# Swapping the fifth and sixth block products of a pair, and moving part of a split from ScalarE to VectorE

## The chip, the cores and the metric

The kernel runs on one core of a Trainium2 chip. The metric is the device time of one execution in microseconds (us). The core has five engines with a queue each, worked off in order: TensorE (PE; its weight loads are shown apart as PEld), VectorE (DVE), ScalarE (ACT), GpSimd (POOL) and SyncE (SP, which only issues DMAs here). Engines wait for one another by semaphores. Each instruction stands in its engine's queue in the order in which the program wrote it, in the stages that matter here, so an instruction that waits holds up all that is behind it on its engine.

## The reference

One decoder block on a sequence of 2048 positions and 1024 channels:

```
h = RMSNorm(x) * (1 + scale(c)) + shift(c)
x_rnn, z_rnn, q, k, v, z_attn, g_r, g_a = split(h @ w_in)          # eight times 1024 columns
xc = causal_conv4(x_rnn);  r, i = sigmoid gates of xc by blocks of 128
a = exp(-8 r softplus(-lam));  hr = scan: hr[t] = a[t] hr[t-1] + sqrt(1 - a^2)[t] i[t] xc[t]
y_rnn  = (hr * silu(z_rnn)) @ w_out_rnn
y_attn = (mixture of three dilated window attentions of rotated q, k and v * silu(z_attn)) @ w_out_attn
out = RMSNorm(x + gate(c) * ((sigmoid(g_r) y_rnn + sigmoid(g_a) y_attn) @ w_o))
```

Results are wanted in float32 accuracy.

## The kernel before, in words

**Split operands.** Every float32 operand of a large matmul is stored as a high part (a rounded copy, float32r) and a low part (operand minus high part), and a product is three matmuls: high x high, high x low, low x high (`mm3`). A high part is made by a copy on ACT (`hi_act`, L162) or DVE (`hi_dve`, L165), a low part by a subtraction on POOL (`lo_pool`, L168) or DVE (`lo_dve`, L171).

**Pairs of column blocks.** The input projection is done in two halves of 1024 positions (f = 0, 1). In each, after the values v, 28 pairs of 128 columns of `w_in` follow (`pair_order`, L1209): pairs 0, 2, 5, 8, 10, 13, 16 and 18 belong to the recurrence (one block of x_rnn and one of z_rnn), those between and up to 21 are gates or plain parts of q and k, 22 to 27 are the rotated and the rest of the plain parts. A pair is a 2 x 2 block product, computed by `strassen` (L351) with seven block products instead of eight. Each block product (`prod`) is twelve matmuls of 128 x 512 into one PSUM tile. Their left operands are made from the pair's raw blocks a11, a21, a22, a12 and two sums s1, s2 (by DVE, `sums`); their right operands B11, T2, T3, T1, B21, T4, B22 are made once for all pairs. In order:

| product | left | right | PSUM tile | what follows |
|---|---|---|---|---|
| 1 | a11 | B11 | X | the pair before gets its seventh product |
| 2 | s2 | T2 | Z | u1 = copy of X (ACT, L390), u2 = Z + u1 (DVE, L391) |
| 3 | a21 | T3 | W | u3 = W + u2 (DVE, L396) |
| 4 | s1 | T1 | V | block (1,1) = V + u3 |
| 5 | a12 | B21 | X again, added | block (0,0) = X |
| 6 | a22 | T4 | Y | block (1,0) = Y + u3 |
| 7 | s2' | B22 | V again, added | block (0,1) = V + u2, one product into the next pair |

The copy u1 is made by DVE (L388) in pairs 5 and 22 of the first half (`COPIED`), else by ACT. Product 5 writes into X and so waits for u1; product 7 writes into V and waits for V + u3.

**The order of the work.** A counter `n_prod` is raised by each product. After a product, `run_late` issues the steps that are due at this count, then `pump` the events of operand making; then `strassen` goes on (u1 and u2 come behind both, after product 2). Operand events (`operand_events`, L267) run four products ahead: a pair's sums are made after product 3 of the pair before, and then one operand is split per product, on ACT and POOL, in the order a11, s2, a21, s1, a12, a22, s2'. The raw blocks are loaded up to six products ahead by SP into five tiles. For the first 20 pairs the split operands of the first half are also stored in HBM (`sD`, seven slots a pair) by DMAs of ACT's queue and loaded from there in the second half, so that the second half splits only those of pairs 20 to 27.

**A finished block's steps.** What is done with a block is counted from the product that finished it (`steps_after`, L232). A gate block gets a sigmoid one product later and a multiplication or a store behind it. Of a recurrent pair, z blocks (1,·) get sigmoid and multiplication (`z_part`, L948); the two x blocks (0,·) get, counted from block (0,0)'s product, for the first and seven later for the second: tap at 0 (ACT), taps at 1 (DVE), split at 2 (ACT, POOL), gates at 5 (PE, six matmuls), sigmoids at 6 (ACT), decay at 7 (POOL, DVE), exponentials at 8 (ACT), root at 9 (DVE), square root at 10 (ACT), scan at 11 (DVE: L1016 multiplies t by gi, L1017 scans), finish and store at 12 (`x_part`, L961: ACT's copy of the last state, L1020, DVE's L1022, SP's store). These reach two and three pairs on.

**Rotary tables.** `piece` (L1082) makes four pieces per half at counts `PIECES` (L43): a copy (DVE, L1087), four transposes 3 products later (PE, L1092), copying out and a store 4 products later. The rotated blocks get shuffle, sines, addition and store with lags that grow with the block's place (`x` in `rotated`).

**Attention and output products.** Attention is woven with the output projections: eight jobs (`steps`) of 64 `mm3` each, four with the recurrence's result (yaT) and then four with attention's (oT). A job's eight input tiles are split by `split_y` (L1768), the high part on ACT, the low part on POOL or DVE, around the end of the job before. Job 0 is split before attention starts, jobs 1 to 4 run in attention, jobs 5 to 7 behind it; then comes the last projection, with seven products per pair again.

Of the kernel before, what the change touches and what calls it, by code (L numbers as in the profile page):

```python
# [14 lines left out]
AF = mybir.ActivationFunctionType  # L15
# [9 lines left out]
NB = 4  # L25
# [10 lines left out]
MORE = 0.8  # L36
FIRST = 4.0
REBUILT = 20
COPIED = (5, 22)
NEG = 1e30  # L40

TABLES = 24
# [50 lines left out]
def decoder_block(ctx, tc, x, c, positions, g_norm, w_mod, b_mod, w_in, b_gate, conv_w, conv_b,  # L93
                  w_a, b_a, w_x, b_x, lam, w_out_rnn, w_out_attn, w_o, g_final, cst, out):
    nc = tc.nc
# [65 lines left out]
    def hi_act(o, i):  # L161
        nc.scalar.activation(o, i, AF.Copy)  # L162
# [49 lines left out]
    def split_s(src):  # L212
        t = s_tile([P, 2, KH, P])
        hi_act(t[:, 0], src)
        lo_pool(t[:, 1], src, t[:, 0])
        return t
# [5 lines left out]
    def run_late(n):  # L222
        for fn in (*late.pop(n, ()), *after_prod.pop(n, ())):
            fn()
        pump()
# [41 lines left out]
    def operand_events(x, pieces):  # L267

        load, v = block_loads(pieces), {}
        tt = nc.vector.tensor_tensor  # L270

        def raw(name, i, half):
            v[name] = load(i, half)

        def split(i, name):
            first[7 * x + i] = t = split_s(v[name])
            if x < REBUILT:
                kept.append((7 * x + i, t))
            if len(kept) > 3 or x >= REBUILT and kept:
                k, t2 = kept.pop(0)  # L280
                nc.scalar.dma_start(sD[k], t2[:].bitcast(F32))

        def sums():
            for name in ("s1", "s2"):
                v[name] = T(wq, [P, KH, P], F32, name, bufs=1)[:]
            tt(v["s1"], v["a21"], v["a22"], ALU.add)
            tt(v["s2"], v["s1"], v["a11"], ALU.subtract)  # L287

        yield -6, lambda: raw("a11", 0, 0)
        yield -5, lambda: raw("a21", 1, 0)  # L290
        yield -4, lambda: raw("a22", 1, 1)
        yield -1, lambda: raw("a12", 0, 1)
        yield 0, sums
        yield 0, lambda: split(0, "a11")
        yield 1, lambda: tt(v["a21"], v["a11"], v["a21"], ALU.subtract)
        yield 1, lambda: split(1, "s2")
        yield 2, lambda: split(2, "a21")
        yield 3, lambda: split(3, "s1")
        yield 4, lambda: split(4, "a12")
        yield 5, lambda: tt(v["s2"], v["a12"], v["s2"], ALU.subtract)  # L300
        yield 5, lambda: split(5, "a22")
        yield 6, lambda: split(6, "s2")

    first, events = {}, []
# [46 lines left out]
    def strassen(f, key, done):  # L351

        up = pu[0]
        x = pair_id[key]
        if f and x == 0:
            for _ in range(NS):
                load_next()
        n_op = iter(range(7 * x, 7 * x + 7))

        def take():  # L360
            if f and x < REBUILT:
                return (f, *loaded.pop(0))
            i = next(n_op)
            return f, i, first.pop(i)

        def prod(ps, b, first, last, op=None):
            f, i, s = op or take()
            bh, bl = B[b]
            for k in range(KH):
                mm3(ps[:], s[:, 0, k, :], s[:, 1, k, :], bh[:, k, :], bl[:, k, :],  # L370
                    first=first and k == 0, last=last and k == KH - 1, skip_group_check=True)
            n_prod[0] += 1
            if f:
                used.add(i)
                while n_loaded[0] - NS in used:
                    load_next()
            run_late(n_prod[0])

        X = T(pj, [P, CH], F32, "X", bufs=2)
        prod(X, "B11", True, False)  # L380
        last_product()
        Z = T(pj, [P, CH], F32, "Z")
        prod(Z, "T2", True, True)
        u1 = T(up, [P, CH], F32, "u1", bufs=1)
        u2 = T(up, [P, CH], F32, "u2", bufs=2)
        with tc.high_priority():
            if not f and x in COPIED:
                nc.vector.tensor_copy(u1[:], X[:])  # L388
            else:
                nc.scalar.activation(u1[:], X[:], AF.Copy)  # L390
            nc.vector.tensor_tensor(u2[:], Z[:], u1[:], ALU.add)  # L391
        W = T(pj, [P, CH], F32, "W")
        prod(W, "T3", True, True)
        u3 = T(up, [P, CH], F32, "u3", bufs=1)
        with tc.high_priority():
            nc.vector.tensor_tensor(u3[:], W[:], u2[:], ALU.add)  # L396
        V = T(pj, [P, CH], F32, "V")
        prod(V, "T1", True, False)
        done(1, 1, V, u3)
        prod(X, "B21", False, True)  # L400
        done(0, 0, X, None)
        Y = T(pj, [P, CH], F32, "Y")
        prod(Y, "T4", True, True)
        done(1, 0, Y, u3)
        op = take()

        def last():
            prod(V, "B22", False, True, op)
            done(0, 1, V, u2)
        behind.append(last)  # L410
# [629 lines left out]
    def rotary_tables(rp, f):  # L1040
# [41 lines left out]
        def piece(q, i):  # L1082

            def repeat():
                src = v[("co", "an")[i]]
                v["rep"] = raw_tile([P, 4, 8, 16]) if f else T(rp, [P, 4, 8, 16], F32, "ev", bufs=3)
                nc.vector.tensor_copy(v["rep"][:], src[:, 4 * q : 4 * q + 4, :].unsqueeze(2).broadcast_to([P, 4, 8, 16]))  # L1087

            def turn():
                v["pt"] = T(pg, [P, 4, P], F32, "pg")  # L1090
                for r in range(4):
                    nc.tensor.transpose(v["pt"][:, r, :], v["rep"][:, r].rearrange("p a b -> p (a b)"), ident)  # L1092

            def store():
                t = raw_tile([P, CH]) if f else T(rp, [P, CH], F32, "ev", bufs=3)
                pt = v["pt"][:].rearrange("p r j -> p (r j)")
                if i == 0:
                    nc.scalar.activation(t[:], pt, AF.Copy)
                else:
                    nc.vector.tensor_scalar(t[:], pt, cs[:, K_SG : K_SG + 1], None, ALU.mult)  # L1100
                nc.sync.dma_start(tabD[f, i, :, q * CH : (q + 1) * CH], t[:])

            return repeat, turn, store
# [6 lines left out]
        assert at_ <= PIECES[0]  # L1110

        for x, (q, i) in enumerate((q, i) for q in range(2) for i in range(2)):
            for d, fn in zip((0, 3, 4), piece(q, i)):
                after_prod.setdefault(base + PIECES[x] + d, []).append(fn)

    def load_tables(qp, f):
# [24 lines left out]
    def rotated_pairs(qp, f, Ct, St):  # L1141

        for base, column, qs in QK:
            def rotated(i, j, ps, u, column=column, qs=qs):
                n = 2 * f + j
                cq = slice(j * CH, (j + 1) * CH)
                t0 = T(qp, [P, CH], F32, "t0", bufs=NT0[f])
                scaled(t0, ps, u, qs)
                v = []

                def shuffle():
                    v.append(T(qp, [P, CH], F32, "t1", bufs=NT1))
                    nc.vector.stream_shuffle(v[0][:], t0[:], swap)
                    nc.gpsimd.tensor_tensor(t0[:], t0[:], Ct[:, cq], ALU.mult)

                def sines():
                    nc.vector.tensor_tensor(v[0][:], v[0][:], St[:, cq], ALU.mult)

                def add():
                    nc.vector.tensor_tensor(v[0][:], v[0][:], t0[:], ALU.add)  # L1160

                def store():
                    for hh in range(4):
                        r0 = (4 * i + hh) * P
                        nc.sync.dma_start(kqT[r0 : r0 + 32, :, column(n) : column(n) + P],
                                          v[0][hh * 32 : (hh + 1) * 32, :].rearrange("p (r j) -> p r j", r=4))


                x = {(1, 1): 0, (0, 0): 1, (1, 0): 2, (0, 1): 3}[i, j]
                steps_after(n_prod[0], ((2, shuffle), (3 + x, sines), (4 + x, add), (5 + x, store)))  # L1170

            strassen(f, (base, "rotated"), rotated)
            yield

    cuts = []
    for t in range(6):
        pieces = []
        i0 = t * P
        while i0 < (t + 1) * P:
            hd, i = divmod(i0, 96)  # L1180
# [547 lines left out]
    def steps(jobs):  # L1728
# [39 lines left out]
        def split_y(j, k):  # L1768
            if j < len(jobs):
                Y[j, k] = yh, yl = [T(fl, [P, CH], F32R, tag, bufs=NY) for tag in ("yh", "yl")]  # L1770
                w, ys, n = jobs[j]
                t = Y0.pop((ys is yaT, n, k))
                hi_act(yh[:], t[:])
                (lo_dve if (k % 2 if j else k > 4) or j > NB + 1 else lo_pool)(yl[:], t[:], yh[:])

        def load_g(t):
# [27 lines left out]
        for t, (j, m) in enumerate(tiles):  # L1804
            ps = T(pj, [P, CH], F32, "pj")
            for k in range(KT):
                x = 2 * t + k // KH
# [25 lines left out]
                yh, yl = Y[j, k]  # L1833
# [5 lines left out]
                x = m * KT + k - KT * (KT - 1)  # L1839
                j1 = j + 1  # L1840
                if m == 0:
                    x, j1 = x + KT * KT, j
# [309 lines left out]
    with tc.manual_schedule():  # L2152
# [10 lines left out]
        for p in range(NP):  # L2163
            for d, fn, args in left_events(p):
                x = 7 * p + d - 4
# [54 lines left out]
```

## Time and profile before

| | us |
|---|---|
| median of 3 runs (2177.54 to 2182.49) | 2177.58 |
| the profiled execution's own time | 2177.2 |
| its span, first to last instruction | 2175.4 |
| PE busy | 2144.5 |
| DVE busy | 1482.4 |
| ACT busy | 1311.0 |
| POOL busy | 1110.7 |

The span runs from the first to the last instruction; the rest of the execution's time lies around it. Busy times are unions of an engine's instructions. Rows of groups read: line, engine, operation, result <- operands, shapes, count | busy time, mean ns of one | idle time ahead of them and what ended it. Rows of waits read: who <- who ended the wait: us in all, how often, the longest. Rows of a timeline read: start, length, engine, line, operation, and in brackets the engine's idle time ahead. The first half's pairs lie at about 120 to 700 us, the second half's at about 790 to 1350, attention at about 1350 to 1880.

### The profile page before, as it was taken

Reading aid. Unit: us, or ns where it says so; the run is one execution under the profiler, and the core shown is the slowest. Engines: PE = TensorE matmul, PEld = TensorE weight load, DVE = VectorE, ACT = ScalarE, POOL = GpSimd, SP = SyncE. Lnnn points to the kernel's source line nnn. Section 1 sums busy time; section 2 is a strip of 40 time slices with the busy share of each in tenths; the row PEclk is TensorE's granted clock in tenths of the full one; section 3 lists DMA queues with packets and bytes.
Section 4 is the critical chain, followed back from the end, with each engine's and each line's share of the span. In section 5 each row is a group of like instructions: output and inputs, shape, how many; then the busy total and the mean of one; then the engine's idle time right before and its main releaser. Section 6 shows DMA issues by size and latency. Waiting matters only on the chain.

```text
span 2175.4 us, 32659 instructions
## 1 busy us (share of the span) xinstructions
PE 2144.5 (99%) x10570; PEld 1788.8 (82%) x10571; DVE 1482.4 (68%) x2570; ACT 1311.0 (60%) x2621; POOL 1110.7 (51%) x868
## 2 busy tenths in 40 slices
PE   9999999999999999999999999999999999999998
PEld 6888788788788888888888887888888988888886
DVE  6769877768656715545546675577767777688887
ACT  5748678568644527457457532688888887444333
POOL 1467677667666323223223575466666674422444
PEclk9999999999999999999999999999999999999999
DMA  8467887787655368898996566988886777898552
GB/s 302 142 213 262 275 300 268 270 285 244 176 116 164 107 230 289 297 307 307 321 327 238 160 165 182 286 270 265 264 269 213 254 235 231 301 320 296 181 172 109
DMA packets 413040, 522.98 MB, mean 240 GB/s; under 512 B 103142, under 2 KB 278466, under 8 KB 411844
## 3 DMA queue, kind: packets, MB, share of 16 engines
q1 hardware_dynamic: 372852, 403.22, 59.2%
q10 hardware_dynamic: 34384, 99.78, 12.3%
q0 software_dynamic: 5632, 17.88, 2.4%
q8 instruction: 84, 1.38, 0.3%
q14 instruction: 88, 0.72, 0.1%
HBM read 332.02 MB, written 188.75 MB: 239 GB/s over the span
## 4 chain that ended last, share of the span: by engine, by line
PE 57%; DMA 4%; DVE 4%; ACT 3%; issue 3%; POOL 2%; SPq 0%; POOLq 0%; ACTq 0%; DVEq 0%
PE X L154 11%; PE V L154 11%; PE pj L154 8%; PE Z L154 6%; PE W L154 6%; PE Y L154 5%; PE sc L154 3%; PE o L154 3%; DMA fg<-gaT 1%; PE pg L154 1%; DMA fg<-mrT 1%; ACT pp L1490 1%; PE pT L1575 1%; DMA vraw<-vN 1%; PE pT L1588 1%
## 5 line engine op out<-in xcount | busy, mean ns | idle before, releaser
L168 POOL TENSOR_TENSOR S<-R,S 128x512 fp32r<-128x512 f32 x192 | 296.0, 1549 | 176.8 <-ACT S L162 85.5
L154 PE MATMUL X<-T,S 128*128 128x512 f32 x1344 | 324.2, 390 | 3.4 <-ACT u L390 1.6
L154 PE MATMUL V<-T,S 128*128 128x512 f32 x1344 | 324.8, 390 | 0.5 <-DVE ev L460 0.2
L154 PE MATMUL pj<-yh,S 128*128 128x512 f32 x896 | 324.2, 403 | 0.0
L154 PEld LDWEIGHTS X<-T,S 128*128 128x128 f32 x1344 | 251.4, 188 | 58.8 <-ACT u L390 3.6
L154 PEld LDWEIGHTS V<-T,S 128*128 128x128 f32 x1344 | 251.4, 188 | 55.6 <-DVE xr L460 1.1
L168 POOL TENSOR_TENSOR S<-s,S 128x512 fp32r<-128x512 f32 x116 | 170.6, 1471 | 149.3 <-ACT S L162 106.4
L154 PEld LDWEIGHTS pj<-yh,S 128*128 128x128 f32 x896 | 168.2, 188 | 30.1 <-DVE S L171 1.1
L154 PE MATMUL pj<-yl,S 128*128 128x512 f32 x448 | 175.8, 392 | 0.4 <-POOL yl L168 0.2
L162 ACT ACTIVATE S<-s 128x512 fp32r<-128x512 f32 x124 | 77.4, 624 | 150.6 <-DVE s L287 104.9
L1490 ACT ACTIVATE pp<-pp,st 128x256 f32<-128x256 f32 (+3 forms) x256 | 133.5, 523 | 54.8 <-DVE st L1489 53.9
L154 PE MATMUL W<-T,S 128*128 128x512 f32 x672 | 162.1, 390 | 0.0
L154 PE MATMUL Y<-T,S 128*128 128x512 f32 x672 | 161.5, 389 | 0.0
L154 PE MATMUL Z<-T,S 128*128 128x512 f32 x672 | 161.4, 389 | 0.0
L162 ACT ACTIVATE S<-R 128x512 fp32r<-128x512 f32 x200 | 121.5, 623 | 59.4 <-issue 15.2
L171 DVE TENSOR_TENSOR ptl<-pT,pth 128x384 fp32r<-128x384 f32 (+1 forms) x160 | 97.9, 629 | 81.7 <-ACT pth L162 79.5
L154 PEld LDWEIGHTS W<-T,S 128*128 128x128 f32 x672 | 125.7, 188 | 26.8 <-issue 0.9
L154 PEld LDWEIGHTS Z<-T,S 128*128 128x128 f32 x672 | 126.1, 188 | 26.2
L154 PEld LDWEIGHTS Y<-T,S 128*128 128x128 f32 x672 | 126.1, 188 | 26.1
L168 POOL TENSOR_TENSOR s<-R,s 128x512 fp32r<-128x512 f32 x32 | 44.3, 1386 | 186.4 <-ACT s L162 166.6
L979 DVE SCALAR_TENSOR_TENSOR xc<-xr,par,xc 128x512 f32<-128x512 f32 x96 | 103.2, 1075 | 53.2 <-ACT xc L973 50.9
L1555 ACT ACTIVATE pp<-pp,M 128x256 f32<-128x256 f32 (+3 forms) x256 | 118.1, 523 | 7.5 <-DVE M L1678 7.3
(424 smaller groups left out, 4939.6 us busy)
## 6 DMA issues: line engine op xcount, KB each, us to landing
sD<-S ACTq DMA_DIRECT2D x140, 512.0 KB, 3.6
S<-sD SPq DMA_DIRECT2D x140, 512.0 KB, 5.2
S<-wD SPq DMA_DIRECT2D x82, 512.0 KB, 5.4
R<-in_w_in_dram SPq DMA_DIRECT2D x144, 256.0 KB, 3.3
wD<-s ACTq DMA_DIRECT2D x64, 256.0 KB, 4.7
kraw<-kqT SPq DMA_DIRECT2D x32, 384.0 KB, 5.1
T<-in_w_mod_dram SPq DMA_DIRECT2D x16, 512.0 KB, 8.9
vN<-ev SPq DMA_DIRECT2D x32, 256.0 KB, 2.6
```

Of the source, the lines that this page charges most:

```text
L154: nc.tensor.matmul(o, lhsT=l, rhs=r, start=st, stop=sp, **kw)
L162: nc.scalar.activation(o, i, AF.Copy)
L168: nc.gpsimd.tensor_tensor(o, i, h.bitcast(F32), ALU.subtract)
L171: return nc.vector.tensor_tensor(o, i, h.bitcast(F32), ALU.subtract).ins
L979: nc.vector.scalar_tensor_tensor(xc, xr[:, i : i + CH], cw(i), xc, ALU.mult, ALU.add)
L1490: nc.scalar.activation(pdst, pdst, AF.Exp, bias=m_, scale=-1.0, accum_out=l_)
L1555: nc.scalar.activation(pp, pp, AF.Copy, scale=w)
L1575: nc.tensor.transpose(pt[:, c0 + j * P : c0 + (j + 1) * P], pp[i][:, k * P : (k + 1) * P], ident)
L1588: nc.tensor.transpose(pt[:, c * P : (c + 1) * P], pp[:, half * P : (half + 1) * P], ident)
```

## The change

The swap: product T4 (Y) is now the fifth and B21 (X) the sixth, with their blocks' steps. The operands are split in the same new order, a22 ahead of a12, and so stored and loaded in that order. The exception of pairs 5 and 22 goes, all copies u1 are ACT's. The rotary pieces' transposes and stores come at 2 and 3 products instead of 3 and 4, and the table of the rotated blocks' places follows the new order. In attention the high parts of the inputs of jobs 1 to 4 are copied by DVE.

```diff
-COPIED = (5, 22)
...
-        yield 4, lambda: split(4, "a12")
+        yield 4, lambda: split(4, "a22")
         yield 5, lambda: tt(v["s2"], v["a12"], v["s2"], ALU.subtract)
-        yield 5, lambda: split(5, "a22")
+        yield 5, lambda: split(5, "a12")
...
         with tc.high_priority():
-            if not f and x in COPIED:
-                nc.vector.tensor_copy(u1[:], X[:])
-            else:
-                nc.scalar.activation(u1[:], X[:], AF.Copy)
+            nc.scalar.activation(u1[:], X[:], AF.Copy)
             nc.vector.tensor_tensor(u2[:], Z[:], u1[:], ALU.add)
...
         done(1, 1, V, u3)
-        prod(X, "B21", False, True)
-        done(0, 0, X, None)
         Y = T(pj, [P, CH], F32, "Y")
         prod(Y, "T4", True, True)
         done(1, 0, Y, u3)
+        prod(X, "B21", False, True)
+        done(0, 0, X, None)
...
-            for d, fn in zip((0, 3, 4), piece(q, i)):
+            for d, fn in zip((0, 2, 3), piece(q, i)):
...
-                x = {(1, 1): 0, (0, 0): 1, (1, 0): 2, (0, 1): 3}[i, j]
+                x = {(1, 1): 0, (1, 0): 1, (0, 0): 2, (0, 1): 3}[i, j]
...
-                hi_act(yh[:], t[:])
+                (hi_dve if 0 < j < NB + 1 else hi_act)(yh[:], t[:])
```

## The prediction

> **What bounds the kernel now.** I read the page first, then the busy time by stretches, then who waits for whom in the first half's products, and last one turn of that loop instruction by instruction. Numbers are us of the one profiled execution, whose own time is 2177.2 (span 2175.4, 1.8 around it); the median of the runs shown is 2177.58, so sums made against 2177.2 stand for it within 0.4.
>
> ```profile
> span 2175.4 us, 32659 instructions
> PE 2144.5 (99%) x10570; PEld 1788.8 (82%) x10571; DVE 1482.4 (68%) x2570; ACT 1311.0 (60%) x2621; POOL 1110.7 (51%) x868
> ```
> ```profile
> 130.00:572.00 442.00, 436.87 (x1914) 356.21 (x1913) 349.04 (x369) 309.13 (x498) 310.32 (x206) 1.00 0.76 261
> ```
> ```profile
> 1000.00:1200.00 200.00, 200.00 (x890) 165.34 (x889) 105.53 (x130) 123.78 (x191) 65.77 (x49) 1.00 0.86 293
> ```
>
> TensorE is busy 99%, so a gain can only be a few waits; a loss has no such limit, if another engine becomes slower than TensorE. The columns of the two stretches are length, then PE, PEld, DVE, ACT, POOL. The first is pairs 0 to 21 of the first half, where every operand is split: DVE 79%, ACT 70%, POOL 70% busy. The second lies in the second half, whose operands mostly come back from HBM: PE never idle, DVE 53%. Their PE waits, first half:
>
> ```profile
> PE X L154 <- ACT u L390: 1.6, 2, 1.4
> PE X L154 <- DVE u L388: 1.3, 1, 1.3
> ```
> ```profile
> PEld X L154 <- ACT u L390: 3.6, 5, 1.8
> PEld V L154 <- DVE xr L460: 1.1, 2, 0.6
> ```
>
> The fifth product adds to X, and waits until the copy u1 of X is made (L390, L388). These waits are at most 6.5, and five times PE stood there: u1 is already as late as it may be. Why it is late shows in one turn, from pair 20's u1 to pair 21's. ScalarE, then VectorE (start, length):
>
> ```profile
> 547.85 0.58 ACT L390 ACTIVATE u<-X 128x512 f32<-128x512 f32 x1
> ...
> 553.79 0.63 ACT L162 ACTIVATE S<-s 128x512 fp32r<-128x512 f32 x1 [3.12 <-DVE s L287]
> 555.60 0.72 ACT L1246 ACTIVATE ev<-ev,par 128x512 f32<-128x512 f32 x1 [1.17 <-DVE ev L460]
> ...
> 568.54 0.58 ACT L390 ACTIVATE u<-X 128x512 f32<-128x512 f32 x1
> ```
> ```profile
> 545.34 1.18 DVE L1016 TENSOR_TENSOR t<-t,gi 128x512 f32<-128x512 f32 x1
> 546.56 2.21 DVE L1017 TENSOR_TENSOR_SCAN y<-a,htail,t 128x512 f32<-128x512 f32 x1
> 548.69 0.66 DVE L391 TENSOR_TENSOR u<-Z,u 128x512 f32<-128x512 f32 x1
> 549.27 1.46 DVE L1022 TENSOR_TENSOR zs<-y,zs 128x512 f32<-128x512 f32 x1
> ...
> 553.07 0.69 DVE L287 TENSOR_TENSOR s<-s,R 128x512 f32<-128x512 f32 x1
> ...
> 554.88 0.69 DVE L460 TENSOR_TENSOR ev<-V,u 128x512 f32<-128x512 f32 x1
> ...
> 565.66 0.69 DVE L1016 TENSOR_TENSOR t<-t,gi 128x512 f32<-128x512 f32 x1 [3.77 <-ACT t L1012]
> 566.39 2.19 DVE L1017 TENSOR_TENSOR_SCAN y<-a,htail,t 128x512 f32<-128x512 f32 x1
> 569.15 0.69 DVE L391 TENSOR_TENSOR u<-Z,u 128x512 f32<-128x512 f32 x1 [0.56 <-ACT u L390]
> ```
>
> The two engines play ping-pong. u1 (ACT) releases u2 (DVE L391); behind u2 come the recurrence's finish (L1022) and the next pair's sums (L287); the sums release ACT's split S, the sum of V (554.88) releases ACT's sigmoid at 555.60, and from there ACT works without a gap to the next u1 at 568.54. One turn takes 568.54 - 547.85 = 20.69. The scan (L1016, L1017) lies outside the loop: at 566.39 it runs ahead of u2, while ACT still works towards u1.
>
> ```profile
> 578.17 2.72 PE X L154 x12
> ```
> TensorE's turn is seven products of 2.72 (twelve matmuls each), 19.04, and in most pairs six matmuls more for the recurrence's gates, 1.36: 20.4. So the loop is as long as TensorE's turn; it has nothing to give.
>
> **The change part by part.** *Order of products.* The sixth product (Y) comes ahead of the fifth (X). X's sum and all that hangs on it, the whole recurrence (tap, taps, split, gates, sigmoids, decay, exponentials, root, square root, scan, finish, store), is counted from there and moves one product later; the rest of a pair's steps (u1, u2, the sums, V's sum, the splits' places) does not move. Within a turn the scan was issued after the second product ahead of u2; now it is issued after the third, behind u2 and **ahead of the sums**. The finish moves behind the sums, but stays ahead of V's sum. So the way u1, u2, ..., V's sum, sigmoid, ..., u1 has all that it had, and the scan with its product as well.
>
> ```profile
> L1017 DVE TENSOR_TENSOR_SCAN y<-a,htail,t 128x512 f32<-128x512 f32 x16 | 33.4, 2085 | 0.6
> L1016 DVE TENSOR_TENSOR t<-t,gi 128x512 f32<-128x512 f32 x16 | 16.7, 1044 | 27.0 <-ACT t L1012 19.6 <-POOL xl L168 7.4
> ```
> ```profile
> ACT S L162 <- DVE s L287: 59.8, 18, 6.9
> ...
> ACT S L162 <- PE X L154: 12.0, 2, 7.7
> ...
> ACT htail L1020 <- DVE y L1017: 10.6, 7, 2.6
> ```
> ```profile
> L955 ACT ACT_TABLE_LOAD x5 | 6.4, 1283 | 0.1
> ```
>
> There are 16 scans between pairs 2 and 21: 16 x (1.044 + 2.085) = 50.1 enter the loop. Off go 10.6, by which scans already ran past u1 (ACT's htail, issued right behind u1, waited for them). Off go three table loads of 1.28, 3.8: in the three turns where a recurrent pair meets the exponentials of the one before, its sigmoids no longer come between exponential and square root. Off go 4.3, ACT's wait for TensorE in the middle (12.0 less the 7.7 at pair 0, ahead of any scan), which a late ACT fills. 50.1 - 10.6 - 3.8 - 4.3 = 31.4.
>
> ```profile
> 130.24 0.59 ACT L390 ACTIVATE u<-X 128x512 f32<-128x512 f32 x1
> ```
> ```profile
> 569.17 3.02 PE L154 MATMUL X<-T,S 128*128 128x512 f32 x12 [1.35 <-ACT u L390]
> ```
> From pair 0's u1 to pair 21's were 568.54 - 130.24 = 438.3; now 469.7, so pair 21's u1 ends at 130.24 + 469.7 + 0.58 = 600.5. X's second product, one product later in the order, stood without that at 569.17 + 2.72 = 571.9. **TensorE is 28.6 late** there; the reserve of one product is in this sum. It is an estimate by hand from these rows. Ends: -6.5 (no lengthening, and X's waits gone), and +36 (V's sum ends 555.57 - 548.43 = 7.1 behind u1, with a scan between 10.2, and at pair 21 the seventh product, which needs it, follows X's by 2.72: 7 more). Nearest to the rows is the middle: the loop is unbroken in every turn that I followed. In the second half the same scans move, but there ACT and DVE have idle time (62% and 53% busy) and most splits are absent: 0, at most +10, since the 3.1 of a scan fits into u1's added 2.72 nearly whole.
>
> *Riders.* A recurrent pair's second z sum now wants its buffer one product behind the store of the one three before it, instead of three: three turns a half may wait for that DMA, 0 to +6, taken 0 because Y's sum itself has products of reserve. The two copies u1 by VectorE become ACT copies: one of them, 0.58, lies in the loop and is left out. The store of the recurrence on SP's queue moves past the load of a pair's first raw block by one place; that block is loaded six products ahead, 16 us, which hides it. Raw blocks and sD slots are the same bytes in the same rhythm, a12 has one product more to land: 0. The rotary pieces' transposes come one product earlier behind their copies. One such copy was late already:
>
> ```profile
> PE pg L1092 <- DVE ev L1087: 0.8, 1, 0.8
> ```
> Its buffer comes free a product earlier too, as the piece's store moves along: 0, at most +2.7 each for two. The order of the rotated tiles' sines keeps each place its lag: 0.
>
> *High parts on VectorE.* 32 copies (jobs 1 to 4, eight each) leave ACT and go to DVE.
>
> ```profile
> L1087 DVE COPY ev<-co x2: 1508/1512/1516, 388.7 to 450.4; 128x512 f32<-128x512 f32 x2
> L1087 DVE COPY ev<-an x2: 426/444/462, 407.5 to 471.6; 128x512 f32<-128x512 f32 x2
> L1087 DVE COPY R<-co x2: 416/966/1516, 1044.9 to 1104.1; 128x512 f32<-128x512 f32 x2
> L1087 DVE COPY R<-an x2: 418/418/419, 1059.8 to 1120.2; 128x512 f32<-128x512 f32 x2
> ```
> ```profile
> sum 126.00, PE 119.20 PEld 104.16 DVE 89.28 ACT 107.62 POOL 89.58; mean PE 29.80 PEld 26.04 DVE 22.32 ACT 26.91 POOL 22.40
> ```
> ```profile
> DVE yl L171 <- ACT yh L162: 17.1, 9, 3.5
> ```
> ```profile
> PE sc L154 <- DVE st L1489: 3.9, 4, 2.4
> PE pT L1575 <- DVE ptl L171: 2.4, 3, 1.3
> PE pT L1575 <- ACT pp L1555: 2.0, 5, 0.9
> ```
> A copy of this size on DVE takes 0.42 or 1.51, over the eight rows' copies (1508, 1516, 426, 462, 416, 1516, 418, 419) 0.84. The splits lie in four stretches, 126 in all (the sum row), with 36.7 of DVE idle; 32 x 0.84 = 26.9 fits, and 17.1 of DVE's waits for ACT's high parts go. PE's waits on these engines in attention are 8.3; I take half, **-4**. Ends: -8.3, and +11.6 if every copy takes 1.51 (48.3 into 36.7).
>
> [...]
>
> **Sum.** 28.6 - 4 = 24.6; 2177.2 + 24.6 = 2201.8, forecast **2202**.
>
> **The rivals.** (1) *The added reserve wins* (other side, faster). X's second product now starts a product, 2.72, later against u1. If the turns' lengthening is hidden, because u1 does not really wait for u2's followers, u1 is never late: X's 6.5 go, and attention's 4: 2167. For it: the waits named are exactly X's. Against it: ACT's waits for DVE's sums, 3.12 in the turn above, lie inside the loop. It decides when the loop grows by less than 2.72 in all between two places where ACT catches up. (2) *Mostly given back*: in the four recurrent pairs between 2 and 21 whose turn has no exponentials, ACT lacks three table loads (3.85) and four activations (each about u1's 0.58, 2.3); if all of that becomes catching up, 4 x 6.15 = 24.6 of the 28.6 are given back, and attention's 4 cancel the rest: 2177. For it: the turns are that uneven. Against it: the 438.3 holds these short turns already, and u1 was late again behind each. (3) *Dearer*: 36 for the loop, 11.6 for the copies and 6 for the z buffers: 2177.2 + 53.6 = 2231.
>
> **How the numbers follow.** Slower through the loop 0.67; dearer (above 2216) 0.08; mostly given back 0.13; reserve wins 0.12. The forecast case by itself spans 2186 to 2216. Measuring this kernel can tell about 0.3%, 6.5 us, from no change: faster is below 2171, slower above 2184. Rival 1 lies below; rival 2 within; the others above: 0.12, 0.13, 0.75. The range leaves out rival 1's and rival 3's tails: 2171 to 2216.
>
> **What would show it.** In the changed profile, first half: scan and its product between u2 and the sums; turns from u1 to u1 of about 22 to 24 where they were 20.7; ACT's wait S<-DVE s (59.8 before in this stretch) longer by tens of us; PE waiting at X for u1, or at V for DVE, by 25 to 35 in all, and the second half as before. Attention: DVE's waits for yh gone, copies of 0.42 and 1.51. It would be wrong if PE's waits at X vanish while the scan stands behind u2: then the sums did not hold up u1. It would also be wrong if the loss sits in the second half or in attention.

## The result and the profile after

The changed kernel takes 2235.8 us (median of four runs, 2234.16 to 2238.48) against 2178.16 for the kernel before (four runs, 2177.54 to 2182.49). The ratio is 1.026, 95% interval 1.0247 to 1.0274: 57 slower. The forecast was 2202, 25 slower; the direction was right, the size less than half, and the time lies above the range. The profiled execution took 2235.1, its span is 2233.3, so the two spans differ by 57.9.

The page of the changed kernel, busy time of each engine:

```profile
span 2233.3 us, 32655 instructions
...
PE 2154.3 (96%) x10570; PEld 1795.6 (80%) x10571; DVE 1509.3 (68%) x2600; ACT 1288.0 (58%) x2585; POOL 1111.2 (50%) x868
```

TensorE has the same 10570 matmuls and fell from 99% to 96% busy. Its longest waits, over the whole span (total, times, longest):

```profile
PE V L153 <- DVE xr L456: 21.6, 9, 5.3
PE V L153 <- DVE ev L456: 21.2, 9, 5.8
PE sc L153 <- DVE st L1485: 5.4, 4, 2.2
PE pg L1088 <- DVE ev L1083: 4.5, 3, 2.5
PE V L153 <- DVE zs L456: 3.6, 2, 2.8
```

The waits at X for u1 (2.9 before) are gone. In their place TensorE waits 46.4 at V (0.2 before, in the pairs): the fourth product of a pair may write V only when VectorE has read the seventh product of the pair before out of it (L456), and the seventh product may add to V only when the first sum has been read. (Lines of the changed file are 4 lower than before from the middle on: L456 is the old L460.)

The pairs 0 to 21 of the first half, the stretch that the prediction read at 130 to 572:

```profile
130.00:612.00 482.00, 444.74 (x1927) 361.58 (x1925) 343.74 (x366) 307.91 (x498) 309.06 (x206) 0.99 0.69 240
```

It is 40 longer; TensorE idles 37.3 in it (482.00 - 444.74), 5.1 before. VectorE and ScalarE are busy as long as before (343.74 and 307.91, before 349.04 and 309.13). So nobody works more; the engines wait for one another. Now one turn, pair 20's u1 to pair 21's, as the prediction read it; ScalarE, then VectorE:

```profile
585.06 0.58 ACT L386 ACTIVATE u<-X 128x512 f32<-128x512 f32 x1
585.53 0.62 ACT L161 ACTIVATE S<-R 128x512 fp32r<-128x512 f32 x1
589.35 0.20 ACT L1016 ACTIVATE htail<-y 128x1 f32<-128x1 f32 x1 [3.19 <-DVE y L1013]
591.38 0.63 ACT L161 ACTIVATE S<-s 128x512 fp32r<-128x512 f32 x1 [1.83 <-DVE s L286]
...
595.15 0.72 ACT L1242 ACTIVATE ev<-ev,par 128x512 f32<-128x512 f32 x1 [1.99 <-DVE ev L456]
...
608.11 0.58 ACT L386 ACTIVATE u<-X 128x512 f32<-128x512 f32 x1
```
```profile
585.67 0.69 DVE L387 TENSOR_TENSOR u<-Z,u 128x512 f32<-128x512 f32 x1 [4.56 <-ACT u L386]
586.28 0.81 DVE L1012 TENSOR_TENSOR t<-t,gi 128x512 f32<-128x512 f32 x1
587.12 2.19 DVE L1013 TENSOR_TENSOR_SCAN y<-a,htail,t 128x512 f32<-128x512 f32 x1
589.24 0.66 DVE L1247 SCALAR_TENSOR_TENSOR ev<-sg,ev 128x512 f32<-128x512 f32 x1
589.82 0.68 DVE L285 TENSOR_TENSOR s<-R,R 128x512 f32<-128x512 f32 x1
590.59 0.69 DVE L286 TENSOR_TENSOR s<-s,R 128x512 f32<-128x512 f32 x1
...
594.44 0.68 DVE L456 TENSOR_TENSOR ev<-V,u 128x512 f32<-128x512 f32 x1
...
608.72 0.69 DVE L387 TENSOR_TENSOR u<-Z,u 128x512 f32<-128x512 f32 x1 [6.13 <-ACT u L386]
```

The loop is there as forecast: u1, u2, product and scan, sums, ScalarE's split S, V's sum, ScalarE's sigmoid, u1. The turn is 608.11 - 585.06 = 23.05, before 20.69. Its back part, from the sigmoid to the next u1, is 12.96 (595.15 to 608.11); before it was 12.94 (555.60 to 568.54). All of the 2.4 sits in the front part, where the scan now stands: 10.09 from u1 to sigmoid, before 7.75. Before, VectorE did the scan while ScalarE was still on its way to u1; now it idles there (6.13), and ScalarE idles while VectorE scans (3.19 at htail, then 1.83 and 1.99).

Where the 57.9 arise, from u1 to u1 (idle: stretch less PE's busy time; clock: in slices of 4, one less the granted clock, times the slice, added up; a part of it falls into idle time, so the two don't add up to the loss):

| stretch | before: length, idle, clock | after: length, idle, clock |
|---|---|---|
| pair 0's u1 to the first of the second half | 660.9, 5.8, 0 | 703.4, 43.2, 8.6 |
| from there to the last u1 of the second half | 541.4, 0, 0 | 553.2, 8.1, 3.4 |

The two stretches are 42.5 and 11.8 longer. Of the rest, 2.1 lie ahead of pair 0's u1 (132.34 against 130.24) and 1.6 behind the last u1 of the second half.

The clock was not in the prediction. After the longest waits TensorE comes back at half the clock. In the windows the clock is the first number behind POOL's busy time:

```profile
612.00:616.00 4.00, 0.00 (x0) 0.00 (x0) 3.91 (x6) 0.83 (x2) 1.48 (x1) 0.92 0.00 0
616.00:620.00 4.00, 2.43 (x6) 1.97 (x7) 2.12 (x3) 2.45 (x5) 1.50 (x2) 0.50 0.67 197
620.00:624.00 4.00, 4.00 (x15) 3.21 (x14) 1.20 (x2) 1.50 (x3) 2.63 (x3) 0.73 0.79 204
624.00:628.00 4.00, 4.00 (x20) 3.30 (x19) 0.09 (x1) 2.41 (x5) 3.15 (x3) 1.00 0.86 255
```
```profile
608.95 2.90 PE L153 MATMUL X<-T,S 128*128 128x512 f32 x12
617.57 5.13 PE L153 MATMUL V<-T,S 128*128 128x512 f32 x12 [5.72 <-DVE ev L456]
```

That is pair 21's seventh product: 5.72 late, and then 5.13 long where twelve such matmuls take 2.90 in the row above it.

### The profile page after: what moved, and what is told of

The parts are those of the page before. It is cut to its first block, busy times and chain, and to the rows that moved or that the text cites. A ratio compares the mean times of both kernels' runs of the same rounds, so it can differ in the third digit from the quotient of the medians.

```text
span 2233.3 us, 32655 instructions
## 1 busy us (share of the span) xinstructions
PE 2154.3 (96%) x10570; PEld 1795.6 (80%) x10571; DVE 1509.3 (68%) x2600; ACT 1288.0 (58%) x2585; POOL 1111.2 (50%) x868
## 5 line engine op out<-in xcount | busy, mean ns | idle before, releaser
L167 POOL TENSOR_TENSOR S<-R,S 128x512 fp32r<-128x512 f32 x192 | 286.9, 1502 | 260.7 <-ACT S L161 109.7
L153 PE MATMUL V<-T,S 128*128 128x512 f32 x1344 | 334.3, 399 | 46.5 <-DVE xr L456 21.6
L153 PEld LDWEIGHTS V<-T,S 128*128 128x128 f32 x1344 | 256.5, 192 | 108.1 <-ACT S L161 27.8
L153 PE MATMUL X<-T,S 128*128 128x512 f32 x1344 | 315.6, 390 | 0.5 <-ACT ev L858 0.5
L167 POOL TENSOR_TENSOR S<-s,S 128x512 fp32r<-128x512 f32 x116 | 181.4, 1564 | 128.7 <-ACT S L161 121.5
L387 DVE TENSOR_TENSOR u<-Z,u 128x512 f32<-128x512 f32 x56 | 38.7, 691 | 195.3 <-ACT u L386 148.7
L975 DVE SCALAR_TENSOR_TENSOR xc<-xr,par,xc 128x512 f32<-128x512 f32 x96 | 115.5, 1203 | 59.4 <-ACT xc L969 57.1
L153 PEld LDWEIGHTS W<-T,S 128*128 128x128 f32 x672 | 126.0, 188 | 26.9 <-issue 0.9
```

The costliest lines, as they stand in the source:

```text
L153: nc.tensor.matmul(o, lhsT=l, rhs=r, start=st, stop=sp, **kw)
L167: nc.gpsimd.tensor_tensor(o, i, h.bitcast(F32), ALU.subtract)
L975: nc.vector.scalar_tensor_tensor(xc, xr[:, i : i + CH], cw(i), xc, ALU.mult, ALU.add)
```

## The experiments

Theories. **A**: the scan's new place, behind u2 and ahead of the sums, lengthens the loop; that is the whole cause. **B**: the rest of the recurrence (taps to root), one product later, stands ahead of V's second sum on VectorE and holds TensorE at V. **C**: it is the new order of products itself. All ratios are against the kernel before on the same chip; us are the ratio less one times 2178. The edits are cut to the steps that change. In the kernel before, `start` counts from X's fifth place, in the changed one from its sixth.

**Only the high parts on VectorE, order of products as before.**

```
-                hi_act(yh[:], t[:])
+                (hi_dve if 0 < j < NB + 1 else hi_act)(yh[:], t[:])
```


> The kernel before with only the high parts of jobs 1 to 4 on VectorE; the products in their old order. The prediction: 4 faster, 2174, bounds -8.3 and +11.6. The trace of the changed kernel, in which TensorE's stretch of attention is 1.6 longer and its waits on DVE's row statistics went from 3.9 to 5.4: -1 to +2, 2177 to 2180.

Measured: 2178.86, ratio 1.0003 (0.9995 to 1.0012), 0 within 2.6. The copies cost a little less than the prediction gave them, which had 0.84 for one and 26.9 for all (here from the changed kernel):

```profile
L164 DVE CAST yh<-R 128x512 fp32r<-128x512 f32 x32 | 23.3, 733 | 0.0
```

They fit into VectorE's idle time, and nothing comes back for it: TensorE's waits at the row statistics rise from 3.9 to 5.3, those at ptl fall from 2.4 to 1.3, one at kq grows from 1.5 to 2.9. In attention, TensorE's waits for these engines do not hang on ScalarE's high parts.

**The changed kernel with the recurrence in its old places.**

```
-            steps_after(start[0] + 7 * j, (
+            steps_after(start[0] - 1 + 7 * j, (
```


> The changed kernel with every step of the recurrence (from taps to store) one product earlier against X's sum, so in the places it had before; the sixth product stays in front of the fifth. If the place of the recurrence is the cause (theories A and B): the 58 go almost whole, 2172 to 2186. If the order of the products itself is (V, Y and X's sums in another rhythm, X's reserve, the operands' order: theory C): 2220 to 2236. In between, 2190 to 2215, would give each a share.

Measured: 2183.99, ratio 1.0019 (1.0010 to 1.0029), +4. Of 57, 53 go: C is small. Of the little that stays, 1.6 lie ahead of pair 0's u1 (131.79 against 130.24). In the first half's pairs, 2.2 longer than before, TensorE has waits of a new kind, the gates' for their low parts, and some at V:

```profile
PE pg L153 <- POOL xl L167: 5.0, 5, 1.2
PE V L153 <- DVE ev L456: 3.4, 2, 2.0
```

X's sum comes one product later here, and the gates' place is the old one, so the steps between them, POOL's split among them, have a product less. That these waits are the rest of the 4 is not shown.

**The kernel before with the recurrence one product later.**

```
-            steps_after(start[0] + 7 * j, (
+            steps_after(start[0] + 1 + 7 * j, (
```


> The kernel before with every step of the recurrence one product later; the products in their old order, X's sum where it was. Theories A and B (place of the recurrence): 2215 to 2240. Theory C (order of the products): 2174 to 2186.

Measured: 2225.32, ratio 1.0211 (1.0197 to 1.0225), +46, with no product swapped. From here the swap adds 11 (1.026 - 1.0211, with some 4 of uncertainty), and not 4 as by the run before: what the order of products costs depends on what it is added to.

**The kernel before with only scan, finish and store one product later.**

```
-                (GATES + 3, exponentials), (GATES + 4, root), (GATES + 5, square_root), (GATES + 6, scan),
-                (GATES + 7, finish), (GATES + 7, store)))
+                (GATES + 3, exponentials), (GATES + 4, root), (GATES + 5, square_root), (GATES + 7, scan),
+                (GATES + 8, finish), (GATES + 8, store)))
```


> The kernel before with only the scan and its product, the finish and the store one product later: behind u2 and ahead of the next pair's sums, as the prediction has it; taps to square root stay. Theory A (the scan in the ping-pong of ACT and DVE is the whole cause): 2205 to 2236, and u1 from pair 0 to pair 21 takes 465 to 480 instead of 438. Theory B (the root, one product later, stands ahead of V's last sum on DVE and waits there for ACT's exponentials): 2175 to 2188, since root and exponentials stay.

Measured: 2217.01, ratio 1.0179 (1.0164 to 1.0195), +39. Pair 0's and pair 21's u1 in its trace:

```profile
130.42 0.59 ACT L390 ACTIVATE u<-X 128x512 f32<-128x512 f32 x1
...
600.98 0.58 ACT L390 ACTIVATE u<-X 128x512 f32<-128x512 f32 x1
```

That is 470.6; the prediction's sum for the scan in the loop was 469.7. But TensorE lost more than u1 did: the first u1 of the second half is 35.5 further behind pair 0's than before. Its waits over the span:

```profile
PE V L154 <- DVE ev L460: 13.0, 8, 3.8
PE pg L154 <- POOL xl L168: 7.7, 5, 2.5
...
PE V L154 <- DVE zs L460: 3.4, 3, 1.8
PE X L154 <- ACT u L390: 3.2, 4, 2.3
```

TensorE waits at X for u1 no more than before (3.2 against 2.9), although X's second product has its old place here; it waits at V, which VectorE's sums free, and at pg. So A holds for most of the loss; what is late at TensorE is V and not X.

**The changed kernel with only square root, scan, finish and store early.**

```
-(GATES + 5, square_root), (GATES + 6, scan), (GATES + 7, finish), (GATES + 7, store)
+(GATES + 4, square_root), (GATES + 5, scan), (GATES + 6, finish), (GATES + 6, store)
```


> The changed kernel with only square root, scan, finish and store one product earlier (scan ahead of u2 again); taps to root stay one product late, the sixth product stays in front of the fifth. If the costs add up: 2235.8 less the 38.9 that the scan cost alone, 2194 to 2200. If the rest of the recurrence and the order of the products cost something only because the loop through the scan is already longer than TensorE's turn: near the run with the whole recurrence early, 2180 to 2190. If the scan is not what costs in this kernel: above 2215.

Measured: 2197.21, ratio 1.0079 (1.0064 to 1.0094), +17. The scan's place is worth 39 here as well (1.026 - 1.0079), so its cost adds to the others'. The rest of the recurrence costs 13 here (1.0079 - 1.0019; in the kernel before it was 7, 1.0211 - 1.0179, each with some 4 of uncertainty), and the trace shows B's mechanism, V's last sum behind late work. TensorE's waits and VectorE around one of them:

```profile
PE V L153 <- DVE xr L456: 10.2, 4, 5.3
```
```profile
255.71 4.43 DVE L975 SCALAR_TENSOR_TENSOR xc<-xr,par,xc 128x512 f32<-128x512 f32 x3 [2.73 <-ACT xc L969]
260.06 2.62 DVE L1065 SCALAR_TENSOR_TENSOR an<-kk,an 128x128 f32<-128x128 f32 x2
262.61 1.75 DVE L299 TENSOR_TENSOR s<-R,s 128x512 f32<-128x512 f32 x1
264.27 1.02 DVE L456 TENSOR_TENSOR xr<-V,u 128x512 f32<-128x512 f32 x1
```

The three taps start only when ScalarE has X's sum ready, and V's sum, which does not need them, stands behind them and behind two products of the rotary tables.

**The same, with taps and split early too (gates to root still late).**

```
-                (0, tap), (1, taps), (2, split), (GATES, gates), ...
+                (0, tap), (0, taps), (1, split), (GATES, gates), ...
```


> The changed kernel with the scan back ahead of u2 and with taps and split of the recurrence one product earlier as well; gates, sigmoids, decay, exponentials and root stay one product late. It stands between the run with only the scan early (2197.2) and the run with all early (2184.0). If the late taps are what cost the 13 (three VectorE instructions, 4.4 in all, right ahead of V's last sum, for which TensorE waited 10.2): 2180 to 2187; and below 2184 if TensorE's 5.0 of waits for the gates' low parts go. If late exponentials and root are what cost them: 2192 to 2198.

Measured: 2189.64, ratio 1.0047 (1.0031 to 1.0064), +10. It falls between the two answers: about 7 of the 13 are the taps', about 6 are the steps' from gates to root, each with 4 to 5 of uncertainty. TensorE's waits at pg for POOL are gone, those at V stay (4.6 for ev, 4.4 for xr, 3.9 for S). So B has no single culprit.

**The same, high parts on ScalarE again.**

> The same kernel with all high parts on ScalarE again: the swap with everything of the recurrence that cost time in its old place. Nothing but TensorE's few waits can be gained: it waited 5 in the first half's pairs of the kernel before. 2174 to 2184, within 3 of the run with the high parts on VectorE.

Measured: 2189.77, ratio 1.0046 (1.0030 to 1.0062): as with the high parts on VectorE, and 10 slower than before, not within 2184 as expected.

**The swap alone, high parts on ScalarE.**

> The changed kernel without the move of the high parts: the swap alone. The kernel before lost 0.3 by that move, with ends of -1.1 and 2.6: 2232 to 2238.

Measured: 2238.04, ratio 1.0267 (1.0251 to 1.0282), as the whole change within its interval. The high parts have no share in the loss.

**Only the root one product later, in the kernel before.**

```
-(GATES + 4, root)
+(GATES + 5, root)
```


> The kernel before with only the root one product later (from the product behind the sums of the pair's X to the next; square root and scan stay, so the square root comes right behind the root). Root ahead of V's last sum as the cause of TensorE's waits at V: +5 to +15, 2184 to 2194. Taps as the cause: 2176 to 2183.

Measured: 2183.55, ratio 1.0013 (1.0003 to 1.0024), +3: on the edge between both answers; the root alone is not B.

**The rotary pieces at their old distances.**

```
-            for d, fn in zip((0, 2, 3), piece(q, i)):
+            for d, fn in zip((0, 3, 4), piece(q, i)):
```


> The changed kernel with the rotary pieces' transposes and stores at their old distances (3 and 4 products behind the copy instead of 2 and 3). TensorE waited 4.5 for the copies there: 2229 to 2233 if those waits are TensorE's own loss, 2234 to 2238 if TensorE only waits there for what it would wait for at V anyway.

Measured: 2236.28, ratio 1.0260 (1.0238 to 1.0282). The 4.5 of waits at the pieces' copies are gone in its trace, and the time is the same: those waits cost nothing. TensorE idles 39.1 instead of 43.2 in the first half, but its clock loses 17.1 there instead of 8.6.

**One more VectorE product behind each scan, in the old place and in the new one.**

```
                 nc.vector.tensor_tensor_scan(y, v["a"][:], t, htail[:, m : m + 1], ALU.mult, ALU.add)
+                nc.vector.tensor_tensor(t, v["a"][:], v["gi"][:], ALU.mult)
```


> The kernel before with one more VectorE product of 128x512 right behind each scan, in the scan's old place ahead of u2; its result goes into a dead tile, so the output is the same. Loop theory: the scan's place lies outside the loop with about 0.5 of slack to u2, so of each 0.69 to 1.04 at most a half counts: 0 to +8, 2178 to 2186. If VectorE's sum of work is what limits: 16 in the first half and 16 in the second at 0.7 to 1.04 each, +22 to +33, 2200 to 2212.

> The same extra VectorE product behind each scan, in the kernel before with scan, product, finish and store one product later (2217.0 without the extra). Loop theory: now it lies in the loop, and each of the first half's 16 counts whole, 0.69 to 1.04: +11 to +17, 2228 to 2234. If the loop were not what limits: as much as the same extra costs in the scan's old place.

Measured: old place 2195.3, ratio 1.0068 (1.0052 to 1.0084), +15; new place 2233.65, ratio 1.0247 (1.0232 to 1.0263), against 1.0179 without it also +15. The extra takes 0.98:

```profile
L1018 DVE TENSOR_TENSOR t<-a,gi 128x512 f32<-128x512 f32 x32 | 31.5, 984 | 1.1
```

In the new place the expectation held (one extra takes 0.83 there). In the old one it fell: I had taken the slack of the one turn that I followed (0.5) for all. In the kernel before, 8 of the 16 scans of pairs 2 to 21 end 0.01 to 2.57 behind u1, and the other 8 only 0.43 to 1.09 ahead of its end. One of the first kind, in which u1 (0.58 from 194.64) is done at 195.22 and u2 starts at 197.69:

```profile
193.80 1.74 DVE L1016 TENSOR_TENSOR t<-t,gi 128x512 f32<-128x512 f32 x1 [2.70 <-POOL xl L168]
195.57 2.19 DVE L1017 TENSOR_TENSOR_SCAN y<-a,htail,t 128x512 f32<-128x512 f32 x1
197.69 0.66 DVE L391 TENSOR_TENSOR u<-Z,u 128x512 f32<-128x512 f32 x1
```

With those 16 distances an extra of 0.98 should give 11.2 (8 x 0.98, and 3.3 from the others); u1 of pair 21 came 13.6 later. So the scan's old place is outside the loop only as long as nothing is added to it. As both places cost the same, this pair of runs does not tell the loop from a loop that the old place is part of. It does speak against VectorE's sum of work as the limit: that was to cost 22 to 33, and in the second half the same 16 extras cost nothing up to the last u1 (14.0 behind at its start and at its end).

**The scan two and three products later, in the kernel before.** With one product later the scan stands ahead of the sums and of V's first sum, with two behind the sums, with three behind both.

```
-(GATES + 6, scan), (GATES + 7, finish), (GATES + 7, store)
+(GATES + 8, scan), (GATES + 9, finish), (GATES + 9, store)      two later
+(GATES + 9, scan), (GATES + 10, finish), (GATES + 10, store)    three later
```


> The kernel before with the scan and its product two products later than before, finish and store with it: behind the sums, still ahead of V's first sum. In the run with one product later it cost 38.9 ahead of both. If the sums (and with them ScalarE's split S) close the loop: 2180 to 2195. If V's sum (and ScalarE's sigmoid behind it, V's reuse) closes it as well: 2205 to 2225. If the scan costs by being late, whatever stands behind it: above 2217.

> The kernel before with the scan and its product three products later than before, finish and store with it: behind the sums and behind V's first sum, ahead of the taps and Y's sum. Loop theory: nothing on the way from u2 to the next u1 waits for it, 2176 to 2192, although it is later than in any other run. If lateness of the recurrence is what costs: above 2217.

Measured: two later 2208.36, ratio 1.0134 (1.0117 to 1.0151), +29; three later 2194.66, ratio 1.0071 (1.0056 to 1.0086), +15. (Of the first, only the times are used.) The later the scan, the smaller the loss, 39, 29, 15: lateness is not what makes the 39. What stands behind the scan does: taking the sums out from behind it gives back 10, V's first sum another 14. The last 15 are more than I expected, and the two answers were 2192 at most or above 2217. Here lateness does cost: pair 21's u1 comes 14.2 further behind pair 0's than before, and ScalarE's gate sigmoid waits for the product with gi, whose tile has one buffer:

```profile
ACT gi L992 <- DVE t L1016: 36.5, 8, 5.9
```

Whether that wait is the whole 15 was not tried.

## Why the prediction was right in direction and wrong in size

- *The bound* (ScalarE and VectorE in ping-pong, no slack against TensorE): right. The scan's place alone costs 39, in both kernels.
- *The loop's 31.4*: the scan does lengthen the chain of u1, but that the run with the scan alone meets the sum so closely (470.6 against 469.7 from pair 0 to pair 21) is partly luck. The 3.8 for three table loads are in the sum, and that run still has all 64 of them in this stretch, as before; without that term the sum for it is 473.5. The loads do go in the changed kernel (61), and there the same stretch is 608.11 - 132.34 = 475.8, 37.5 longer and not 31.4, since taps to root add to it.
- *"X's second product, one product later in the order, stood without that at 569.17 + 2.72 = 571.9. TensorE is 28.6 late there; the reserve of one product is in this sum"*: **the step that failed.** The reserve is real, X's waits vanished, but TensorE does not come as far as X: it stands at V. The stretch from pair 0's u1 to the first u1 of the second half is 42.5 longer, which is 5.0 more than the chain of u1 up to pair 21 and not 2.7 less; the 5.0 arise between pair 21's u1 and the next, where the wait of 5.72 at V stands. So of the 13.9 between 28.6 and 42.5, 2.7 are the reserve that brought nothing, 6.1 the chain and 5.0 what stands behind it. The end "+36", which reckoned with V, was on paper; I chose the middle, because in the rows before TensorE's waits were at X. They were at X because that was the tightest place then, not because it would stay so.
- *The rest of the recurrence at nothing*: wrong. Its steps were moved past V's second sum and priced only by what they free on ScalarE. They cost 13 in the changed kernel, 7 in the kernel before.
- *The order of products at nothing*: 4, or 11 where the recurrence is late already.
- *Second half, 0 to +10*: 12. The reason given, that most operands come back from HBM, holds for TensorE up to pair 19, by whose u1 it has idled 1.3. From pair 20 on the operands are split again, and there it idles 6.8 more; the longest wait is 5.8, for V, at 1282.7.
- *The clock*: not in the sum at all. 8.6 + 3.4 in the two halves, 1.7 in attention. Inside the loop it only takes the place of waiting: the swap alone has 13.7 of it in the first half against 8.6 here, 39.0 idle against 43.2, and is as long within 1.7. Behind the last long wait of each half, where TensorE sets the pace again, it counts as far as TensorE is busy in it: 2.3 and 2.5 of the 3.4 each.
- *Attention, -4*: 0 within 2.6. The copies were priced nearly right (23.3 for 26.9); that half of TensorE's waits hung on ScalarE's high parts was a guess.
- *Riders*: the z buffers' waits came, at VectorE: 3.4 in three turns of the first half and 16.6 in three of the second, the longest 6.9. They cost little: with the scan early they are 11.8 in the second half, and that half is only 1.5 longer than before. The rotary waits came too (4.5), and cost nothing by the run above.
- *Rivals*: "the added reserve wins" was right that X's waits go, and wrong that nothing takes their place. The dearer case had the time nearly right (2231) by luck: its 36 for the loop are right in kind, but the other 17.6 were for copies and z buffers, where the runs show the late recurrence and the second half.
- *The signs named*: turns of 22 to 24 came on the average (22.7, from 20.6 to 26.3). The sign of being wrong came as well: X's waits vanished with the scan behind u2, and yet the sums do hold up u1. It was badly chosen, since V stops TensorE before X can. The copies of 0.42 came (18 of 32), the others spread up to 2.07. ScalarE's wait for the sums was to grow and fell (59.8 to 32.8 over the stretch); the scan is met one instruction earlier, at htail (10.6 to 46.2), which stands ahead of that split on ScalarE.

No version of the swap beat the kernel before. The most that could be had in the first half is what TensorE idles there, 5.8, less than the 6.5 that a measurement tells.

## What to carry to other kernels

When two engines pass work back and forth at the pace of the third, look for each instruction in the gap between them: what stands ahead of the partner's input can cost up to its full length every turn (here 39 for 16 scans of 3.1 in the first half, 50 in all), what is done while the partner works costs nothing as long as it ends before the partner does, and the same instruction moved by one place can change from the one to the other. Take the slack from all turns, not from the one that was followed. And when the tightest wait gets a reserve, price the next tightest on the same engine: the gain ends there.

## What the runs showed of the hardware

Waits of TensorE had a second price in these runs. From pair 0's u1 on the clock was 1.00 in every slice of the kernel before, up to its last few us. In the changed kernel it is 0.50 for a while behind each of the waits of 4.3, 5.3, 5.7 and 5.8, and behind one of 2.2 in attention (at 1833): for 3.41 from 202.31 and from 1833.88, for 6.83 from 270.58, from 615.32 and from 1280.92, so each dip cost 1.7 or 3.4. Shorter waits did it too, and not always: in the run with the scan alone waits of 1.9 (at 233) and 2.5 (at 196) had a dip of 1.7 each, while in the changed kernel waits of 2.6 to 2.8 (at 156, 258 and 493) had none.

Within each run all dips start on one grid of 3.41: in the changed kernel the five starts lie 68.27, 344.74, 665.60 and 552.96 apart, which is 20, 101, 195 and 162 times 3.4133. The dips go with TensorE's idle time within one interval of this grid:

| run, wait | its length | idle in the intervals that it falls into | clock after it |
|---|---|---|---|
| changed kernel, at 156 | 2.69 | 1.07, 1.62 | 1.00 |
| swap alone, at 156 | 2.73 | 2.70 in one | 0.50 |
| changed kernel, at 258 | 2.83 | 1.70, 1.13 | 1.00 |
| changed kernel, at 493 | 2.64 | 1.62, 1.02 | 1.00 |
| scan alone, at 196 | 2.52 | 0.25, 2.27 | 0.50 |
| scan alone, at 233 | 1.86 | 1.86 in one | 0.50 |
| scan alone, at 306 | 1.62 | 1.62 in one | 1.00 |

The first two rows are nearly the same wait in nearly the same kernel; one is cut by the grid and the other is not. Over 15 profiles (all but that of the scan two products later), from pair 0's u1 to 20 us before the end, 59 intervals at full clock had 1.9 or more of idle time, and each was followed by an interval at half clock. Of the 50 with 1.5 to 1.9, 9 were, and of the more than 8800 with less none. So in these runs a dip came behind every interval in which TensorE idled 1.9 or more of the 3.41 and behind none in which it idled less than 1.5, and waits of up to 2.8 passed free where the grid cut them.
